# Attention scores with keys on partitions, 512 queries wide, in a one-core decoder layer on Trainium2

## Chip, cores and metric

The kernel runs on 1 core of one Trainium2 chip. The metric is device time in microseconds (us), the median of a kernel's runs. TensorE (PE) multiplies matrices and PEld is its weight load; VectorE (DVE) and ScalarE (ACT) work element by element; GpSimd (POOL) does small work and starts some DMAs; SyncE (SP) starts the others.

## The reference

One decoder layer over 2048 tokens of width 1024, in float32. An input projection feeds two mixers; the change concerns the attention of 8 heads (query and key of 96 numbers, of which 64 are per head and 32 carry the position; value of 64):

```python
h = jnp.einsum('bsd,dn->bsn', x, w_in[l]) + b_in[l]
for start in range(0, seq, Q_BLOCK):
    end = start + Q_BLOCK
    s = jnp.einsum('bqhd,bkhd->bhqk', q[:, start:end], k[:, :end]).astype(jnp.float32) * scale
    causal = jnp.arange(end)[None, :] <= (start + jnp.arange(Q_BLOCK))[:, None]
    p = jax.nn.softmax(jnp.where(causal, s, -jnp.inf), axis=-1)
    outs.append(jnp.einsum('bhqk,bkhd->bqhd', p.astype(v.dtype), v[:, :end]))
```

The attention output is gated by SiLU, the other mixer is a gated spatial unit, both are projected, gated, added, projected again and normalised.

## The kernel before

Every float32 product runs as three passes of the type float32r: `split` (lines 64 to 66) makes a 12-bit head of an operand on ACT (`hi`) and the remainder on DVE (`lo`), and hi·hi, hi·lo and lo·hi add up in one PSUM bank (`mm3`).

Four stages follow each other. Stage 1 makes q, k and v of all tokens and stores their heads and remainders in DRAM; stage 2 makes the mixed v of the spatial unit; stage 3 is attention; stage 4 gates, merges, projects and normalises (lines 774 to 873). The gates' own projections (`gates`, lines 493 to 568, tile `psg`) are cut into steps of three 512-wide products. The first 48 steps run ahead of stage 3, all others between the steps of the attention, as filling work that depends on nothing of it.

Stage 3 (from line 575) goes through 64 blocks of 256 queries of a head (`Block`). A block has three kinds of steps. `score` (line 619) puts 128 queries on the partitions and up to 512 keys in columns of a bank `pss`, three passes each; DVE adds the causal mask and takes each row's maximum (lines 631 to 639); when a row of 128 queries is complete, ACT takes the exponential with the maximum as its bias and adds up the row (line 642). `turn` (line 648) transposes the probabilities on TensorE, two key tiles and 256 queries at a time, into the bank `pt`, and `split` turns them into `ph` and `pl`. `product` (line 670) multiplies these with V, whose 128 columns hold head and remainder, into `po`; lines 684 to 686 add the two halves and send the block to DRAM. The row sums stay in `ls`; after all blocks they are turned, inverted and written to `rd` (lines 756 to 764), and stage 4 loads them back as `r` and multiplies (lines 816 to 818).

The order on TensorE is written by a loop (lines 715 to 754) that models when each step's input should be ready; `FILL` sets how much gates' work stands between. Within stage 3 TensorE keeps that order, and every engine takes its own instructions in the order in which they stand:

```python
            elif turned and turned[0][0] <= now and (blocks[vi].kv > 0 or o_free <= now):
                cost = blocks[vi].product(lo)
            elif ti < si and ti <= vi + 1 and done_s[ti] <= now and t_ready <= now and len(turned) < 2:
                cost = blocks[ti].turn()
            elif si < len(order) and si <= ti + 1 and banks and banks[0] <= now:
                cost, last = blocks[si].score()
            if cost:
                credit += cost * FILL
            else:
                next(fill, None)
```

Loads of Q (lines 603 and 604), K and V (lines 588 to 590) and gates' weights (`fst`, line 498) share SP's queue; POOL starts the stores `gd` and `otd`.

Of the kernel before, what the change touches and what calls it, by code (L numbers as in the profile page):

```python
# [19 lines left out]
ALU = mybir.AluOpType  # L20
# [13 lines left out]
W = 512           # width of each mixer  # L34
C = 512           # tokens of a chunk
# [6 lines left out]
# inv_freq[i] = 10000 ** (-2 i / 32) in float32  # L42
# [10 lines left out]
LAG_S, LAG_E, LAG_H, LAG_T, LAG_O = 1500.0, 700.0, 1500.0, 2100.0, 1500.0  # L53
FILL = 1.19       # time of the gates' products per time of the attention's
# [3 lines left out]
def hybrid_layer_kernel(ctx, tc, xT, x, pos, invf, w_lat, b_lat, w_v, b_v,  # L58
# [41 lines left out]
    rd = dram.tile([H, S], F32, name="rd")  # L100

    # ----------------------------------------------------------- constants
# [7 lines left out]
    # keep where q - k >= 0  # L110
# [7 lines left out]
    # x^T, two chunks of tokens on chip, each as (hi, lo)  # L118
# [22 lines left out]
    # ======================================================= 1: q, k and v  # L141
# [10 lines left out]
    # latent weights, with the first chunk of x  # L152
# [20 lines left out]
    # rope tables: cos, sin of pos * inv_freq for all tokens  # L173
# [24 lines left out]
    # cos(r) = sin(pi/2 - |r|)  # L198
# [6 lines left out]
    # up projections, with the rms gains (and the score scale) folded in  # L205
# [8 lines left out]
    tc.keep_in_program_order(dve.tensor_scalar(gq, gq, SCALE, None, op0=ALU.mult))  # L214
    for t in range(3):
# [11 lines left out]
    def rope(dst, src, t0, n, heads, nm):  # L227
        """dst[P, n*heads, 32] = rope(src); tables of token tiles t0 .. t0+n"""
# [16 lines left out]
    def latent(c, ts):  # L245
        """latents of token tiles ts: bias, rms norm, rope of k"""
# [44 lines left out]
    def up(c, lh, ll):  # L291
        """k, v and q of a chunk, in four parts"""
# [4 lines left out]
        evict(pk, DR, krd[:, :, tok])  # L297
# [11 lines left out]
        for t in range(4):  # L309
            tk = slice(t * P, (t + 1) * P)  # L310
            # q rope
# [8 lines left out]
            # k nope, head pairs  # L320
# [4 lines left out]
            # v  # L325
# [10 lines left out]
            # q nope, head pairs  # L336
# [24 lines left out]
    # ============================== 2: v of the spatial gating unit, mixed  # L361
    with ExitStack() as ph:
# [12 lines left out]
        def gelu_v(c, t):  # L375
            """gelu(v) of a token tile and its mean and variance"""
# [21 lines left out]
        # the first tiles along with the last part of phase 1  # L398
# [27 lines left out]
            # [s, g, t]: keep t >= s  # L426
# [148 lines left out]
    with ExitStack() as ph:  # L575
# [17 lines left out]
        class Block:  # L593
# [4 lines left out]
            def __init__(self, h, qc, hds):  # L598
# [6 lines left out]
                if h not in hds:  # L605
                    hds[h] = head(h)
# [108 lines left out]
        while vi < len(order):  # L715
# [3 lines left out]
            elif turned and turned[0][0] <= now and (blocks[vi].kv > 0 or o_free <= now):  # L719
                lo = len(turned[0]) == 1  # L720
                turned[0].pop(0)
                if lo:
                    turned.pop(0)
# [210 lines left out]
```

## Time and profile before

| | us |
|---|---|
| median of 3 runs | 1771.89 |
| lowest and highest run | 1771.39, 1774.26 |
| span of the profiled execution, first to last instruction | 1775.5 |
| TensorE busy in that span | 1731.4 (98%) |
| VectorE, ScalarE, GpSimd busy | 1094.2 (62%), 754.6 (43%), 134.3 (8%) |

The profiled execution has no time of its own beside its span of 1775.5 us, which is 0.2% above the median of the runs. In the profile, a group of instructions is one line with its engine, operation, tiles (written from left to right as out<-in), shape and count, then busy time, the mean duration of one in ns, and the idle time of its engine just before, with what ended it. Products on TensorE overlap: a 512-wide one lasts some 390 ns, but the next begins sooner, so that their pace is read from the starts in the timeline. The granted clock is a share of 2.4 GHz; 0.5 would be 1.2 GHz throughout.

### The profile page before, as it was taken

How to read it: one execution, taken by the hardware profiler on the slowest of the kernel's cores; microseconds unless marked ns; L12 is line 12 of the kernel's file. 1: busy time of each engine (PE TensorE's matmuls, PEld its weight loads, DVE VectorE, ACT ScalarE, POOL GpSimd, SP SyncE). 2: the span in 40 equal slices, each digit the busy share in tenths (PEclk: the TensorE clock that was granted, in tenths of full speed). 3: DMA queues.
4: the chain of work that ended last, by engine and by line, in shares of the span. 5: the costliest groups of instructions: out<-in, count | busy, mean ns of one | idle time of the engine just before them, and what ended most of it. 6: DMA issues, size and time to landing. Idle time of an engine off the chain costs nothing.

```text
span 1775.5 us, 25048 instructions
## 1 busy us (share of the span) xinstructions
PE 1731.4 (98%) x9249; PEld 1484.1 (84%) x9249; DVE 1094.2 (62%) x2209; ACT 754.6 (43%) x1708; POOL 134.3 (8%) x231
## 2 busy tenths in 40 slices
PE   7999999899999999999999999999999999999998
PEld 7999887788888888888788888888888877888886
DVE  6765686476664555444776666654445478777664
ACT  6533442255544454545655445544544341303020
POOL 0000011100000100000100000100001000000000
PEclk9999999999999999999999999999999999999999
DMA  6564851631321422422713212321123886657341
GB/s 220 194 196 160 276 170 38 181 99 49 101 72 66 140 68 66 119 68 75 215 62 89 76 55 81 122 72 59 60 66 120 283 270 225 215 197 215 120 131 72
DMA packets 111100, 229.06 MB, mean 129 GB/s; under 512 B 13120, under 2 KB 41920, under 8 KB 108608
## 3 DMA queue, kind: packets, MB, share of 16 engines
q1 hardware_dynamic: 99968, 193.88, 34.9%
q0 software_dynamic: 11008, 33.57, 5.4%
q8 instruction: 73, 1.20, 0.3%
q14 instruction: 51, 0.42, 0.1%
HBM read 155.50 MB, written 71.89 MB: 128 GB/s over the span
## 4 chain that ended last, share of the span: by engine, by line
PE 45%; issue 41%; DMA 5%; POOL 4%; DVE 3%; ACT 2%; SPq 0%; POOLq 0%; DVEq 0%; ACTq 0%
PE po L86 11%; PE psg L86 9%; PE psa L86 4%; PE psl L86 4%; PE pb L86 4%; PE pa L86 4%; PE pss L86 3%; PE pt L658 2%; POOL gd L519 2%; DMA wost<-in_w_out_dram 1%; PE psq L86 1%; POOL otd L686 1%; DMA xst<-in_xT_dram 1%; DMA mxd<-mo 1%; PE psr L86 1%
## 5 line engine op out<-in xcount | busy, mean ns | idle before, releaser
L86 PE MATMUL psg<-xh,fwh 128*128 128x512 f32 x896 | 375.3, 419 | 4.9 <-DVE fo L522 4.9
L66 DVE TENSOR_TENSOR pl<-pt,ph 128x512 fp32r<-128x512 f32 (+2 forms) x352 | 199.7, 567 | 287.2 <-ACT ph L65 285.5
L86 PE MATMUL psg<-xl,fwh 128*128 128x512 f32 x896 | 354.5, 396 | 0.0
L86 PE MATMUL psg<-xh,fwl 128*128 128x512 f32 x896 | 354.1, 395 | 0.0
L65 ACT CAST ph<-pt 128x512 fp32r<-128x512 f32 (+2 forms) x352 | 172.0, 489 | 241.4 <-PE pt L658 208.8
L642 ACT ACTIVATE pr<-pss,nm 128x512 f32<-128x512 f32 (+2 forms) x320 | 198.0, 628 | 114.9 <-DVE nm L639 95.9
L86 PE MATMUL pss<-Kh,Q 96*128 96x512 f32 (+3 forms) x640 | 222.5, 377 | 12.9 <-DMA Q<-qrd 7.2
L86 PEld LDWEIGHTS psg<-xh,fwl 128*128 128x128 f32 x896 | 169.6, 189 | 38.4
L636 DVE TENSOR_REDUCE mx<-pss 128x1 f32<-128x384 f32 (+2 forms) x288 | 175.6, 619 | 29.4 <-PE pss L86 26.1
L86 PEld LDWEIGHTS psg<-xh,fwh 128*128 128x128 f32 x896 | 170.6, 190 | 25.6 <-issue 5.3
L86 PEld LDWEIGHTS psg<-xl,fwh 128*128 128x128 f32 x896 | 171.4, 191 | 20.7
L658 PE MATMUL pt<-ident,pr 128*128 128x128 f32 x1088 | 167.2, 274 | 0.0
L86 PEld LDWEIGHTS pss<-Kh,Q 96*128 96x128 f32 x640 | 119.3, 189 | 30.7 <-ACT pr L642 9.7
L658 PEld LDWEIGHTS pt<-ident,pr 128*128 128x128 f32 x1088 | 125.6, 141 | 5.8 <-ACT pr L642 0.4
L86 PEld LDWEIGHTS po<-ph,V 128*128 128x128 f32 x576 | 108.7, 189 | 26.0 <-ACT ph L65 3.2
L86 PE MATMUL pss<-Kl,Q 96*128 96x512 f32 (+2 forms) x320 | 115.9, 362 | 0.0
L86 PE MATMUL po<-pl,V 128*128 128x256 f32 x576 | 113.9, 279 | 0.2
L86 PE MATMUL po<-ph,V 128*128 128x256 f32 x576 | 112.8, 276 | 1.2 <-DVE o L685 0.7
L86 PEld LDWEIGHTS po<-pl,V 128*128 128x128 f32 x576 | 96.5, 190 | 11.3 <-DVE pl L66 1.2
L86 PE MATMUL po<-woh,mh 128*128 128x512 f32 x256 | 100.8, 394 | 1.2 <-ACT mh L65 1.2
L86 PE MATMUL po<-woh,ml 128*128 128x512 f32 x256 | 100.4, 393 | 0.0
L86 PE MATMUL po<-wol,mh 128*128 128x512 f32 x256 | 99.7, 390 | 0.0
(208 smaller groups left out, 2986.3 us busy)
## 6 DMA issues: line engine op xcount, KB each, us to landing
fst<-in_w_feat_dram SPq DMA_DIRECT2D x56, 512.0 KB, 3.7
gd<-fo POOLq DMA_DIRECT2D x96, 256.0 KB, 2.3
wabst<-in_w_ab_dram SPq DMA_DIRECT2D x32, 512.0 KB, 4.2
xst<-in_xT_dram SPq DMA_DIRECT2D x31, 512.0 KB, 4.9
kd<-e SPq DMA_DIRECT2D x16, 512.0 KB, 3.2
vd<-ve SPq DMA_DIRECT2D x16, 512.0 KB, 4.1
qnd<-e SPq DMA_DIRECT2D x16, 512.0 KB, 4.7
Q<-qnd SPq DMA_DIRECT2D x64, 128.0 KB, 2.9
```

What stands on the lines that cost most here:

```text
L65: act.copy(hi, src)
L66: dve.tensor_tensor(lo, src, hi.bitcast(F32), op=ALU.subtract)
L86: inorder(pe.matmul(*args, **kw))
L519: pool.dma_start(gd[c][m], o)
L636: dve.tensor_reduce(self.mx[:, i:i + 1], ps[:, :n], axis=AX.X, op=ALU.max)
L642: act.activation(pr[:, k0:k0 + ne], pe_[:, :ne], AF.Exp, bias=self.nm, accum_out=ls[:, self.h, 2 * self.qc + j, e:e + 1])
L658: inorder(pe.transpose(pt[:, i, j * P:(j + 1) * P], self.pr[j][:, (k + i) * P:(k + i + 1) * P], ident))
L686: pool.dma_start(otd[self.qc // 2][self.h * DV:(self.h + 1) * DV, self.qc % 2 * 256:(self.qc % 2 + 1) * 256], o2)
```

## The change

Stage 3 is rewritten for 32 blocks of 512 queries (8 heads, four chunks c of 512 tokens; the block of chunk c has 4(c+1) key tiles of 128). Each product of the score has 128 keys on the partitions and 512 queries in columns (`score`, bank `pst`), so that the exponential leaves the probabilities as the product with V wants them. The maximum of a query, which lies across partitions there, comes from an earlier product of its own, `top`: heads of q times heads of k, one pass, queries on the partitions, in banks `pss`; DVE masks and reduces it. When all `top` steps of a block are done, DVE spreads the negated maxima on a diagonal (`dg`), `shift` multiplies that with a matrix of ones (bank `pbm`), and ACT writes the result as row 96 of the block's Q; K has a row of ones there (`krd`). The row sums are added on POOL into `acc`, tile by tile; `total` sums them over partitions with another product with ones (bank `pbl`), DVE inverts, scales the block's output and POOL stores it. The path through `rd` and `r` is gone. A block's `top` steps stand between the `score` steps of the block before it.

```diff
-    krd = dram.tile([DR, 2, S], F32, name="krd")
+    krd = dram.tile([DR + 1, 2, S], F32, name="krd")
...
+    one = xs.tile([P, 2, C], F32, tag="st", name="one")
+    dve.memset(one[:1, 0, :], 1.0)
+    dve.memset(one[:1, 1, :], 0.0)
+    for c in range(4):
+        sp.dma_start(krd[DR:, :, c * C:(c + 1) * C], one[:1])
...
+        ps_s = ph.enter_context(tc.tile_pool(name="p3S", bufs=2, space=PSUM))
+        ps_t = ph.enter_context(tc.tile_pool(name="p3T", bufs=2, space=PSUM))
+        ps_b = ph.enter_context(tc.tile_pool(name="p3B", bufs=1, space=PSUM))
...
+            Kt = kp.tile([DH + 1, 2, S], F32R, tag="K", name="K")
...
+            for ks in (slice(0, 512), slice(512, S)):
+                sp.dma_start(Kt[:DN, :, ks].bitcast(F32), kd[h // 2, h % 2 * DN:(h % 2 + 1) * DN, :, ks])
+                sp.dma_start(Kt[DN:, :, ks].bitcast(F32), krd[:, :, ks])
...
+                self.Qt = kp.tile([DH + 1, 2, C], F32R, tag="Q", name="Q")
+                sp.dma_start(self.Qt[:DN].bitcast(F32), qnd[h // 2, h % 2 * DN:(h % 2 + 1) * DN, :, cs])
+                sp.dma_start(self.Qt[DN:DH].bitcast(F32), qrd[h // 4, h % 4 * DR:(h % 4 + 1) * DR, :, cs])
...
+                for j in range(4):
+                    nb = 4 * c + j + 1
+                    ends = [-(-nb * (i + 1) // (c + 1)) * P for i in range(c + 1)]
+                    self.units += [(j, i, k0, k1 - k0, i == c)
+                                   for i, (k0, k1) in enumerate(zip([0] + ends, ends))]
...
+            def top(self):
+                j, i, k0, n, last = self.units.pop(0)
                 ps = ps_s.tile([P, 512], F32, tag="s", name="pss")
...
-                mm(ps[:, :n], Qh, self.Kh[:, ks], start=True, stop=False)
-                mm(ps[:, :n], Qh, self.Kl[:, ks], start=False, stop=False)
-                mm(ps[:, :n], Ql, self.Kh[:, ks], start=False, stop=True)
...
-                        act.activation(pr[:, k0:k0 + ne], pe_[:, :ne], AF.Exp, bias=self.nm,
-                                       accum_out=ls[:, self.h, 2 * self.qc + j, e:e + 1])
...
-                        inorder(pe.transpose(pt[:, i, j * P:(j + 1) * P],
-                                             self.pr[j][:, (k + i) * P:(k + i + 1) * P], ident))
+                mm(ps[:, :n], self.Qt[:DH, 0, j * P:(j + 1) * P], self.Kt[:DH, 0, k0:k0 + n],
+                   start=True, stop=True)
                 with tc.high_priority():
                     if last:
...
+                        dve.tensor_tensor(ps[:, n - P:n], ps[:, n - P:n], mask, op=ALU.add)
+                    dve.tensor_reduce(self.mx[:, j, i:i + 1], ps[:, :n], axis=AX.X, op=ALU.max)
+                    if not self.units:
+                        nm = sm.tile([P, 4, 1], F32, tag="nm", name="nm")
+                        dve.tensor_reduce(nm, self.mx, axis=AX.X, op=ALU.max, negate=True)
+                        self.dg = sm.tile([P, 4, P], F32R, tag="dg", bufs=1, name="dg")
+                        dve.tensor_tensor(self.dg, ident.unsqueeze(1).to_broadcast([P, 4, P]),
+                                          nm.to_broadcast([P, 4, P]), op=ALU.mult)
...
+            def shift(self):
+                pb = ps_b.tile([P, C], F32, tag="b", name="pbm")
+                mm(pb, ones, self.dg.rearrange("p j q -> p (j q)"), start=True, stop=True)
+                with tc.high_priority():
+                    act.copy(self.Qt[DH:, 0, :], pb[DH:DH + 1, :])
...
+            def score(self, k):
+                q0 = max(0, k - 4 * self.c) * P
+                ks = slice(k * P, (k + 1) * P)
+                ps = ps_t.tile([P, C], F32, tag="t", name="pst")
+                mm(ps[:, q0:], self.Kt[:, 0, ks], self.Qt[:, 0, q0:], start=True, stop=False)
+                mm(ps[:, q0:], self.Kt[:DH, 1, ks], self.Qt[:DH, 0, q0:], start=False, stop=False)
+                mm(ps[:, q0:], self.Kt[:DH, 0, ks], self.Qt[:DH, 1, q0:], start=False, stop=True)
+                p = pp.tile([P, C], F32, tag="p", name="p")
+                hi = pp.tile([P, C], F32R, tag="ph", name="ph")
+                lo = pp.tile([P, C], F32R, tag="pl", name="pl")
+                with tc.high_priority():
+                    if k >= 4 * self.c:
+                        dve.tensor_tensor(ps[:, q0:q0 + P], ps[:, q0:q0 + P], maskt, op=ALU.add)
+                    act.activation(p[:, q0:], ps[:, q0:], AF.Exp)
+                    split(p[:, q0:], hi[:, q0:], lo[:, q0:])
+                    if k == 0:
+                        self.acc = sm.tile([P, C], F32, tag="acc", name="acc")
+                        pool.tensor_copy(self.acc, p)
...
+                        pool.tensor_tensor(self.acc[:, q0:], self.acc[:, q0:], p[:, q0:], op=ALU.add)
+                    if k == self.nk - 1:
+                        self.ah = sm.tile([P, C], F32R, tag="ah", bufs=1, name="ah")
+                        self.al = sm.tile([P, C], F32R, tag="al", bufs=1, name="al")
+                        split(self.acc, self.ah, self.al)
...
+            def product(self, k, e):
...
+                mm(self.po[:, q0:], self.Vt[:, k, :], (hi, lo)[e][:, q0:],
+                   start=k == 0 and e == 0, stop=k == self.nk - 1 and e == 1)
+                if k == self.nk - 1 and e == 1:
...
+                        act.copy(o1, self.po[DV:, :])
+                        dve.tensor_tensor(self.o2, self.po[:DV, :], o1, op=ALU.add)
...
+            def total(self):
+                pb = ps_b.tile([P, C], F32, tag="b", name="pbl")
+                mm(pb, ones, self.ah, start=True, stop=False)
+                mm(pb, ones, self.al, start=False, stop=True)
+                r = sm.tile([DV, C], F32, tag="r", bufs=1, name="r")
+                dve.reciprocal(r, pb[:DV, :])
+                dve.scalar_tensor_tensor(self.o2, self.o2, 0.5, r, op0=ALU.mult, op1=ALU.mult)
+                pool.dma_start(otd[self.c][self.h * DV:(self.h + 1) * DV, :], self.o2)
...
-        order = [(h, qc if h % 2 == 0 else 7 - qc) for h in range(H) for qc in range(8)]
...
+        order = [(h, c if h % 2 == 0 else 3 - c) for h in range(H) for c in range(4)]
...
+        def work(cost):
+            credit[0] += cost * rate
+            while credit[0] > 0.5 * STEP_NS:
+                credit[0] -= STEP_NS
+                next(fill, None)
...
+        work(blocks[0].shift())
+        todo, sums = [], []
+        def later():
+            if len(todo) > 2:
+                n, k = todo.pop(0)
+                b = blocks[n]
+                work(b.product(k, 0))
+                work(b.product(k, 1))
+                if k == b.nk - 1:
+                    sums.append(n)
+            elif sums:
+                work(blocks[sums.pop()].total())
...
+        for n in range(len(order)):
+            b, nx = blocks[n], blocks.get(n + 1)
+            for k in range(b.nk):
+                work(b.score(k))
+                todo.append((n, k))
+                if sums:
+                    work(blocks[sums.pop()].total())
+                later()
+                if nx:
+                    want = min(nx.nu, -(-nx.nu * (k + 1) // max(1, b.nk - 1 - b.nk // 5)))
+                    while nx.nu - len(nx.units) < want:
+                        work(nx.top())
+            if nx:
+                work(nx.shift())
+            block(n + 2)
+        while todo:
+            n, k = todo.pop(0)
+            work(blocks[n].product(k, 0))
+            work(blocks[n].product(k, 1))
+        work(blocks[len(order) - 1].total())
...
-                for e in range(2):
-                    sp.dma_start(r[e * DV:(e + 1) * DV, :], rd[2 * f + e, tok].partition_broadcast(DV))
-                dve.tensor_tensor(o, o, r, op=ALU.mult)
```

TensorE in stage 3, before, where probabilities are turned; `psg` is a gates' product, `pt` a transpose of probabilities `pr`, `po` a product with V:

```order
L86 MATMUL po<-ph,V 128x256 x2
L86 MATMUL po<-pl,V 128x256 x2
L658 MATMUL pt<-ident,pr 128x128 x4
L86 MATMUL psg<-xh_2940,fwh 128x512
L86 MATMUL psg<-xl_2941,fwh 128x512
```

Between a gates' step and the products with V stands a turn of four transposes.

TensorE after the change, some steps within a block; `pst` is a score with keys on partitions, `pss` a `top` product of the next block:

```order
L86 MATMUL pst<-Q,K 128x512 x3
L86 MATMUL psg<-xh_2972,fwh 128x512
L86 MATMUL psg<-xl_2973,fwh 128x512
L86 MATMUL psg<-xh_2972,fwl 128x512
...
L86 MATMUL po<-ph,V 128x512
L86 MATMUL po<-pl,V 128x512
...
L86 MATMUL pss<-K,Q 128x512 [waits DVE_49] x2
```

No transpose of probabilities is left on TensorE, and one-pass products `pss` have come in.

TensorE after the change, at the end of a block without a gates' step behind `pbm`:

```order
L86 MATMUL pst<-Q,K 128x128 [waits Activation_49]
L86 MATMUL pst<-Q,K 128x128 x2
L86 MATMUL po<-ph,V 128x384 [waits Activation_49]
L86 MATMUL po<-pl,V 128x384 [waits DVE_49]
L86 MATMUL psg<-xh_2972,fwh 128x512
L86 MATMUL psg<-xl_2973,fwh 128x512
L86 MATMUL psg<-xh_2972,fwl 128x512
L86 MATMUL pbm<-dg,ones 128x512 [waits PE_49]
L86 MATMUL pst<-Q,K 128x512 [waits DVE_49,Activation_49]
```

ACT at the same place:

```order
L668 ACTIVATE p<-pst 128x128 [waits DVE_49,Pool_49]
L65 CAST ph<-p 128x128 [waits PE_49,Activation_49]
L65 CAST ah<-acc 128x512 [waits Pool_49]
L652 CAST Q<-pbm 1x512 [waits DMAHW7_49,DMAHW0_49,PE_49]
L668 ACTIVATE p<-pst 128x512 [waits PE_49]
```

The first score of the next block waits for ACT's write of Q's row 96 (`Q<-pbm`), and ahead of that on ACT stands the head of the finished sums (`ah`), which waits for POOL.

DVE after the change, in a block of chunk 0, from the inverse of the block before to the diagonal of the next:

```order
L702 RECIPROCAL r<-pbl 64x512 [waits PE_49]
L637 TENSOR_TENSOR pss<-pss,mask 128x128 [waits PE_49]
L667 TENSOR_TENSOR pst<-pst,maskt 128x128 [waits PE_49]
L638 TENSOR_REDUCE mx<-pss 128x1 [waits DVE_49]
L703 SCALAR_TENSOR_TENSOR o_6250<-o_6250,r 64x512
L641 TENSOR_REDUCE nm<-mx 128x4 [waits DVE_49]
L66 TENSOR_TENSOR pl<-p,ph 128x128 [waits Activation_49]
L643 TENSOR_TENSOR dg<-ident,nm 128x512 [waits DVE_49]
```

The inverse stands ahead of the last mask of this block and of the diagonal that `shift` needs.

## Rows read from the trace of the kernel before

**Rows 1.** The profile's page: span, and busy time of each engine.

```profile
span 1775.5 us, 25048 instructions
...
PE 1731.4 (98%) x9249; PEld 1484.1 (84%) x9249; DVE 1094.2 (62%) x2209; ACT 754.6 (43%) x1708; POOL 134.3 (8%) x231
```

**Rows 2.** Busy time by stretch: end of attention, all of it; then stage 4.

```profile
core 0: us, PE busy (x) PEld busy (x) DVE busy (x) ACT busy (x) POOL busy (x), PEclk, DMA share, GB/s
...
1366.00:1411.50 45.50, 45.50 (x203) 37.74 (x203) 23.27 (x34) 15.83 (x25) 4.88 (x9) 1.00 0.87 294
353.60:1411.50 1057.90, 1043.53 (x5745) 904.39 (x5744) 612.32 (x1237) 535.62 (x1307) 85.22 (x156) 1.00 0.30 94
...
1500.00:1700.00 200.00, 200.00 (x880) 164.85 (x879) 143.78 (x221) 41.50 (x54) 8.25 (x9) 1.00 0.57 184
```

**Rows 3.** Groups of TensorE's instructions by shape, 353.6 to 1411.5 us.

```profile
L86 PE MATMUL psg<-xh,fwh 128*128 128x512 f32 x848 | 355.1, 419 | 0.0
...
L658 PE MATMUL pt<-ident,pr 128*128 128x128 f32 x1088 | 167.2, 274 | 0.0
```

**Rows 4.** TensorE's timeline: start, length, instruction, count in the row.

```profile
503.24 0.40 PE L86 MATMUL po<-pl,V 128*128 128x256 f32 x2
503.48 0.60 PE L658 MATMUL pt<-ident,pr 128*128 128x128 f32 x4
503.83 0.48 PE L86 MATMUL psg<-xh,fwh 128*128 128x512 f32 x1
504.15 0.40 PE L86 MATMUL psg<-xl,fwh 128*128 128x512 f32 x1
504.38 0.39 PE L86 MATMUL psg<-xh,fwl 128*128 128x512 f32 x1
504.61 0.34 PE L86 MATMUL pss<-Kh,Q 96*128 96x384 f32 x1
504.79 0.33 PE L86 MATMUL pss<-Kl,Q 96*128 96x384 f32 x1
...
515.95 0.49 PE L658 MATMUL pt<-ident,pr 128*128 128x128 f32 x3
516.19 0.48 PE L86 MATMUL pss<-Kh,Q 96*128 96x512 f32 x1
516.50 0.39 PE L86 MATMUL pss<-Kl,Q 96*128 96x512 f32 x1
```

**Rows 5.** Waits of TensorE, 353.6 to 1411.5 us: total, times, longest.

```profile
PE pss L86 <- DMA Q<-qrd: 7.2, 3, 3.1
PE pss L86 <- ACT pr L642: 5.4, 6, 2.2
```

**Rows 6.** Busy time by stretch around TensorE's longest wait of stage 3.

```profile
608.00:612.00 4.00, 0.87 (x8) 0.67 (x7) 1.12 (x3) 1.00 (x3) 0.54 (x1) 1.00 0.91 242
612.00:616.00 4.00, 4.00 (x13) 3.33 (x12) 1.85 (x4) 1.45 (x4) 0.00 (x0) 0.57 0.15 45
616.00:620.00 4.00, 4.00 (x30) 3.84 (x28) 3.19 (x10) 1.36 (x4) 0.53 (x1) 1.00 0.65 218
```

**Rows 7.** Groups of VectorE's instructions by shape, whole span.

```profile
L66 DVE TENSOR_TENSOR pl<-pt,ph 128x512 fp32r<-128x512 f32 x224 | 154.5, 690 | 227.6 <-ACT ph L65 226.5
...
L631 DVE TENSOR_TENSOR pss<-pss,mask 128x128 f32<-128x128 f32 x128 | 36.7, 293 | 16.2 <-PE pss L86 15.0
...
L763 DVE RECIPROCAL r<-pl 128x128 f32<-128x128 f32 x1 | 1.0, 957 | 1.1 <-PE pl L761 1.1
```

**Rows 8.** Groups of ScalarE's instructions by shape, whole span.

```profile
L65 ACT CAST ph<-pt 128x512 fp32r<-128x512 f32 x224 | 131.2, 586 | 165.5 <-PE pt L658 162.2
...
L65 ACT CAST fwh<-fst 128x512 fp32r<-128x512 f32 x112 | 66.7, 622 | 38.0 <-PE psg L86 37.6 <-DMA fst<-in_w_feat_dram 0.4
...
L642 ACT ACTIVATE pr<-pss,nm 128x128 f32<-128x128 f32 x8 | 2.9, 367 | 3.4 <-DVE nm L634 3.4
```

**Rows 9.** Groups of GpSimd's instructions by shape, whole span.

```profile
L427 POOL TENSOR_SCALAR_AFFINE_SELECT wsst<-wsst 128x1024 f32<-128x1024 f32 x1 | 1.1, 1099 | 20.5 <-DMA wsst<-in_wsT_dram 20.5
L106 POOL TENSOR_SCALAR_AFFINE_SELECT ident<-ident 128x128 f32<-128x128 f32 x1 | 0.3, 292 | 0.6 <-DVE ident L105 0.6
```

More of the change, by code (lines that the diff above doesn't have):

```diff
@@ L52 @@
 MT_ORDER = [m for f in range(4) for m in (MT_U + f, MT_ZB + f, MT_ZA + f)] + list(range(MT_GA, MT))
[L53 to L54 removed]
+MM_NS = 0.45
+STEP_NS = 3 * MM_NS * 512
 @with_exitstack
@@ L581, in hybrid_layer_kernel @@
+        ps_b = ph.enter_context(tc.tile_pool(name="p3B", bufs=1, space=PSUM))
         ps_o = ph.enter_context(tc.tile_pool(name="p3O", bufs=1, space=PSUM))
+        maskt = sm.tile([P, P], F32, bufs=1, name="maskt")
+        dve.memset(maskt, 0.0)
+        pool.affine_select(out=maskt, in_=maskt, compare_op=ALU.is_ge, fill=NEG,
+                           base=0, pattern=[[1, P]], channel_multiplier=-1)
+        ones = sm.tile([P, P], F32R, bufs=1, name="ones")
+        dve.tensor_scalar(ones, ident, 0.0, 1.0, op0=ALU.mult, op1=ALU.add)
@@ L590, in head @@
             sp.dma_start(Vt.bitcast(F32), vd[h])
[L591 removed]
+            return Kt, Vt
         class Block:
[L598 to L617 removed]
@@ L690, in hybrid_layer_kernel @@
-        ls = sm.tile([P, H, NT, 4], F32, tag="ls", bufs=1, name="ls")
-        dve.memset(ls, 0.0)
-        keep[0] = True
-        order = [(h, qc if h % 2 == 0 else 7 - qc) for h in range(H) for qc in range(8)]
-        hds = {}
-        blocks = [None] * len(order)
-        done_s = [0.0] * len(order)
-        si = ti = vi = 0
-        now = credit = 0.0
-        banks = [0.0] * 4
-        row, turned = [], []
-        t_ready = o_free = act_free = 0.0
+                        dve.tensor_tensor(ps[:, n - P:n], ps[:, n - P:n], mask, op=ALU.add)
@@ L706, in block @@
+        keep[0] = True
+        order = [(h, c if h % 2 == 0 else 3 - c) for h in range(H) for c in range(4)]
+        hds = {0: head(0)}
+        blocks = {}
         def block(n):
-            if n < len(order) and blocks[n] is None:
-                h, qc = order[n]
-                if n % 8 == 1 and h + 1 < H:
+            if n < len(order):
+                h, c = order[n]
+                blocks[n] = Block(h, c, hds)
+                if n % 4 == 1 and h + 1 < H:
                     hds[h + 1] = head(h + 1)
-                blocks[n] = Block(h, qc, hds)
@@ L713, in hybrid_layer_kernel @@
-        block(0)
-        block(1)
-        while vi < len(order):
-            cost = 0.0
-            if credit > 0.0:
-                pass
[L719 to L723, printed above, removed]
-                cost = blocks[vi].product(lo)
-                if blocks[vi].kv == blocks[vi].nk:
-                    vi += 1
-                    o_free = now + cost + LAG_O
-            elif ti < si and ti <= vi + 1 and done_s[ti] <= now and t_ready <= now and len(turned) < 2:
-                cost = blocks[ti].turn()
-                t_ready = now + cost + LAG_T
-                turned.append([now + cost + LAG_H, t_ready])
-                if blocks[ti].kt == blocks[ti].nk:
-                    ti += 1
-            elif si < len(order) and si <= ti + 1 and banks and banks[0] <= now:
-                cost, last = blocks[si].score()
-                banks.pop(0)
-                row.append(now + cost)
-                if last:
-                    act_free = max(now + cost + LAG_S, act_free)
-                    for _ in row:
-                        act_free += LAG_E
-                        banks.append(act_free)
-                    done_s[si] = act_free + 200.0
-                    row = []
-                if not blocks[si].todo:
-                    si += 1
-                    block(si + 1)
-            if cost:
-                credit += cost * FILL
-            else:
-                cost = 648.0
-                credit -= cost
-                next(fill, None)
-            now += cost
@@ L757, in hybrid_layer_kernel @@
-        l1 = sm.tile([P, H * NT], F32, tag="l1", bufs=1, name="l1")
-        dve.tensor_reduce(l1, ls.rearrange("p h b i -> p (h b) i"), axis=AX.X, op=ALU.add)
-        dve.tensor_scalar(l1, l1, 2.0, None, op0=ALU.mult)
-        pl1 = ps_t.tile([P, P], F32, tag="t", name="pl1")
-        pe.transpose(pl1, l1, ident)
-        r1 = sm.tile([P, P], F32, tag="r1", bufs=1, name="r1")
-        dve.reciprocal(r1, pl1)
-        sp.dma_start(rd.rearrange("h (b q) -> (h b) q", q=P), r1)
+        cols = sum((4 * c + 2.5) * 4 * P + 3 * C + 5 * (4 * c * C + 1280) for h, c in order)
@@ new lines, in hybrid_layer_kernel @@
+        rate = (len(MT_ORDER) * 4 * 8 - 48 - 24) * STEP_NS / (cols * MM_NS)
+        credit = [0.0]
+        def work(cost):
[3 more added lines that the diff above has]
+                next(fill, None)
+        block(0)
+        while blocks[0].units:
+            work(blocks[0].top())
+            work(300.0)
+        for _ in range(6):
+            next(fill, None)
+        work(blocks[0].shift())
+        todo, sums = [], []
```

109 lines of the change are left out of this document (23 added, 86 removed).

## The prediction

> **What bounds the kernel now.** The page first: TensorE is busy 1731.4 of 1775.5 us and no other engine above 62% [rows 1]. Busy time hides pace, so the stretches come next: attention takes 1057.9 us at a granted clock of 1.00, with VectorE at 612.3 (58%), ScalarE at 535.6 and GpSimd at 85.2 [rows 2]. Its last 45.5 us hold nothing but gates' products. In stage 4 there are 880 products in 200 us, 0.227 each. The timeline gives the paces inside attention from start to start [rows 4]: 0.23 us for 512 columns, 0.17 for 384, 0.12 for 256, and by proportion 0.06 for 128. A turn of four transposes costs 0.67 to the second start behind it, less the 0.23 of the product between: 0.44; one of three costs 0.55 less 0.23, 0.32.
>
> With these, stage 3 adds up so: 3 x 848 gates' products [rows 3] are 585.1 us, the scores (three passes over 139,264 columns) 188.5, the products with V 128.5, the turns (1088 transposes [rows 3], 224 fours and 64 threes) 119.0. That is 1021.1, so 36.8 of the 1057.9 is idle or slow. The list of waits names some of it: 7.2 for Q's loads and 5.4 for the exponential [rows 5]. The longest gap shows the rest: after some 3 us with 8 products the clock of the next 4 us is 0.57, and 13 products run where the following 4 us hold 30 [rows 6]. So a wait of 3 us costs about 2 us more afterwards.
>
> **Columns on TensorE, removed and added.** The transposes go: -119.0. The scores keep their columns (672 products of 512, 96 each of 384, 256 and 128: 188.4) and the V products are 448 of 512 and 64 of each narrower width, 125.6: together -3. New are 320 `top` products in one pass (139,264 columns, 62.9), 32 `shift` (7.4) and 64 `total` (14.7): +85. Net **-37**.
>
> **The old stalls.** They hang on turns and on short blocks. Half as many blocks, each with its Q loaded two blocks ahead, and scores that wait for nothing but two banks should keep about 11 of the 36.8 (late loads, where SP's queue is shared as before). **-26.**
>
> **The added wait at each block's end.** This is the price I trust least, and it decides. The first score of the next block needs row 96 of Q. Ahead of that write ScalarE has the cast `ah`, which needs GpSimd's last add, which needs the last exponential. From the start of the last score, with durations of the nearest rows: 0.35 for its passes to end, mask 0.29 [rows 7], exponential 0.37 [rows 8], GpSimd's add of 128 columns about 0.35 (from 0.29 [rows 9]), cast 0.6, and the write of Q taken like the 0.59 of a PSUM cast [rows 8], with 0.25 for five hand-overs: **2.8 us**. Meanwhile TensorE has the narrow score (0.19), two V products (0.35), three gates' products (0.69) and `pbm` (0.23), 1.46 us; in about half of these 24 boundaries three more gates' products, 2.14. The waits are 1.35 and 0.66: 12 x 1.35 + 12 x 0.66 = **+24**. Bounds: 14, if the Q write of one partition is short, to 48, if the chain takes 3.8.
>
> **Blocks of chunk 0.** They have four key tiles, so between `total` of the block before and their own last `top` lies little. On VectorE the inverse stands ahead of the last mask and of `dg`. An inverse over 128 x 128 took 0.957 us [rows 7]; 0.15 of that taken as fixed, 512 columns take 0.15 + 4 x 0.80 = 3.4. Bounds 1.36 (if half of the partitions counted) to 3.83 (four times). From `total` to `shift` TensorE has 3.7 us of work by the paces; VectorE needs 0.7 for what is before it, 3.4 and 2.6 for masks, reduction, scale, `pl` and `dg`: 6.7. So `shift` waits 2.9 and the score behind it another 0.6: 3.5 for each of seven, **+24.5** (10 to 35), and since gaps this long are followed by half clock [rows 6], **+6**.
>
> **Smaller waits.** Where chunk 1 follows chunk 0 (4 times), `top` steps stand three in a row on two banks, and the third waits for a mask and a reduction, about 1.5: **+6**. The inverse in the other 24 blocks holds reductions that free `pss`: 7 in all (0 to 30). Q's loads still come just in time once or twice: 4, against 7.2 before [rows 5]. Stage 4 loses cover: where 45.5 us of gates' work lay ahead of it [rows 2], only 48 products, 11 us, do now: 4 (0 to 10). Together **+21**.
>
> **Hidden work.** VectorE gets 128 masks more (37 by 0.293), 32 `dg` and 32 scalings like `pl` (22 each by 0.690 [rows 7]), 5 for `nm` and 109 for the inverses: +195, so some 807 us of about 1070, 75%. ScalarE has one exponential and one head for a tile where it had the same, with 32 `ah` and 32 Q writes (38) on top: near 55%. GpSimd gets 320 adds and copies; the nearest rows are selects, 1.099 for 1024 columns and 0.292 for 128 [rows 9]. An add of 512 columns lies between 0.64 (interpolated) and 1.1 (it reads 1024): at most 350 us on an engine that was busy 85. All three stay below TensorE, so nothing for their sums; if VectorE's cover goes, it is case C. The path through `rd` (32 loads, 16 multiplications) goes from stage 4, where nothing waited for it that I count: 0.
>
> The Trainium skill ("GPSIMD Engine Reference", section "Performance versus the Vector engine") gives 2.6 cycles an element at 1.2 GHz for such an add; my estimate from that page is 1.1 us for 512 columns, the upper of my two ends, and no row here shows it. By it the sum would not move, as GpSimd would be at a third.
>
> **Sum.** -37 - 26 + 24 + 24.5 + 6 + 6 + 7 + 4 + 4 = **+12.5**. The sum is made on the span of 1775.5, which is 0.2% above the median of the runs; put on the median of 1771.9 it gives **1784 us**.
>
> **Rivals.** *B: faster, the new waits are covered.* For it: TensorE's columns fall for certain, and of the hand-over's terms only mask and cast are measured on tiles like these. If the chain takes 2.1 us or less, boundaries with six gates' products no longer wait, and the others wait 0.66; if the inverse costs 1.4, chunk 0 waits little. Taking 0.66 at all 24 is 16, with 10 for chunk 0 and 4 for stage 4: 30. -63 + 30 = -33, **1739**. It decides below a chain of 2.1 us and an inverse of 1.5. Against it: five hand-overs over four engines in a row, and 0.957 for a quarter of the columns.
>
> *C: slower, VectorE falls behind for GpSimd.* `pl` had one input in PSUM (`pt`) and one in SBUF; now both, `p` and `ph`, are in SBUF, while GpSimd adds the same `p`. If the two engines can't read at once, a `pl` that becomes ready 0.6 us into an add of 1.1 waits 0.5: 320 x 0.5 = 160 us on VectorE, 967 of 1070 (90%). A key tile has 3.3 us of TensorE work and VectorE would then have 0.3 us free in it; reductions free `pss` late, and the chains at block ends grow by 0.5 to 1 us: 32 x 0.8 = 26, with 14 for `top` steps: **1824**. It decides when the wait per tile exceeds VectorE's free 0.8 us. For it: nothing in the trace of before puts these two side by side. Against: GpSimd would hold the port a third of the time only.
> The Trainium skill ("SBUF — State Buffer", section "Who interferes with whom") states that a VectorE instruction with two SBUF inputs and a GpSimd instruction that reads SBUF lock each other out, the second waiting until the first is done; it is the mechanism of C and speaks against this change. No run here shows it yet; the profile after would, by `pl` instructions longer than 0.69.
>
> *That the transposes stay in some form* is excluded by the order of TensorE after the change.
>
> **Chances and range.** The forecast (A, 1765 to 1805 as its own range): 0.42; B 0.30; C 0.28. The measurement tells some 3.5 us (0.2%) from no change. Of A 0.05 lies below 1768.4, 0.09 within 3.5 of the median, 0.28 above; B is all faster, C all slower: faster 0.35, same 0.09, slower 0.56. For 8 in 10 the range must take in the upper part of B and most of C; with the inverse at 1.36 and the boundary waits at 14 A's sum falls by 25 or more, with 48 and 35 it rises by 35: 1736 to 1832.
>
> **What would show it.** Right: TensorE's waits for ScalarE's Q write and for `dg` sum to 40 to 60 us and lead its list; the inverse lasts 3 us or more; stage 3 is 1060 to 1080 us; the clock dips at the chunk-0 blocks alone. For B: stage 3 under 1035, inverse under 1.5, chain under 2.1. For C: `pl` above 0.9 on average, VectorE above 88%, and waits of TensorE for `mx` spread over the blocks. Wrong altogether: waits on loads or at stage 4 that outweigh these, or paces of `top` products other than 0.23.

## The result, and the profile after

| | before | after |
|---|---|---|
| median of the runs, us | 1772.7 (1771.39 to 1774.26) | 1885.49 (1879.17 to 1894.78) |
| span of the profiled execution, us | 1775.5 | 1877.5 |

The changed kernel is slower: ratio 1.063, 95% interval 1.060 to 1.067. The sign was forecast; the size was not: 12.5 us stood in the sum, 113 were measured, and 1885 lies above the range. The profiled execution is the fastest of the changed kernel's four, so that what follows accounts for 102 of the 113.

The page's first lines answer to [rows 1]: TensorE is busy 93% of the span where it was 98%, VectorE 74% where it was 62%.

```profile
span 1877.5 us, 22826 instructions
...
PE 1742.6 (93%) x8064; PEld 1434.4 (76%) x8064; DVE 1383.8 (74%) x2321; ACT 764.9 (41%) x1388; POOL 486.1 (26%) x520
```

Busy time by stretch (columns as in [rows 2]), cut at the last gates' product as there: attention, then stage 4.

```profile
353.60:1501.00 1147.40, 1045.65 (x4534) 850.18 (x4533) 889.70 (x1327) 539.22 (x977) 435.76 (x443) 0.96 0.25 79
1501.00:1877.50 376.50, 357.56 (x1537) 289.55 (x1535) 256.23 (x388) 79.48 (x102) 15.39 (x17) 0.98 0.57 185
```

Attention is 89.5 us longer (1057.9 before [rows 2]), stage 4 12.5 (364.0 before). The 89.5 can be put together from three things. TensorE stands idle 101.8 us (1147.4 less 1045.7) where it was 14.4: +87. Its granted clock is 0.96 where it was 1.00: attention lost 44 us to half clock, in 20 stretches, where it had lost 5 in three: about +40. And the products that the change saves are the -37 of the forecast. 87 + 40 - 37 = 90. This is rougher than it looks: some 4 us of half clock lie in time that is also counted as idle, the changed attention begins at 345.7 us, so that some 6 us of its products lie ahead of the cut, and about 10 us of busy time stay unexplained.

The waits of TensorE, 353.6 to 1490 us, name the idle time (total, times, longest):

```profile
PE pst L86 <- ACT Q L652: 61.2, 27, 4.0
PE pbm L86 <- DVE dg L643: 20.5, 8, 4.2
PE pss L86 <- DVE mx L638: 11.1, 12, 1.9
PE pbm L86 <- DVE r L702: 6.4, 1, 6.4
PE po L86 <- DVE pl L66: 2.0, 5, 0.9
```

88 of the 101 are the hand-over between blocks (Q's row 96, `dg`, and once the single bank that `pbm` and `pbl` share, which the inverse still read): 86 at the 31 block ends, 2 at the first block's start. Groups by shape, VectorE first, then ScalarE and GpSimd:

```profile
L66 DVE TENSOR_TENSOR pl<-p,ph 128x512 fp32r<-128x512 f32 x224 | 228.6, 1023 | 146.1 <-ACT ph L65 145.0
L66 DVE TENSOR_TENSOR fwl<-fst,fwh 128x512 fp32r<-128x512 f32 x112 | 100.5, 907 | 10.4 <-ACT fwh L65 10.3
L702 DVE RECIPROCAL r<-pbl 64x512 f32<-64x512 f32 x32 | 106.9, 3341 | 1.7 <-PE pbl L86 1.7
L66 DVE TENSOR_TENSOR al<-acc,ah 128x512 fp32r<-128x512 f32 x32 | 22.1, 692 | 11.7 <-ACT ah L65 11.7
...
L652 ACT CAST Q<-pbm 1x512 fp32r<-1x512 f32 x32 | 18.5, 578 | 11.3 <-PE pbm L86 10.7
...
L674 POOL TENSOR_TENSOR acc<-acc,p 128x512 f32<-128x512 f32 x192 | 267.5, 1393 | 320.7 <-ACT p L668 319.6
L674 POOL TENSOR_TENSOR acc<-acc,p 128x128 f32<-128x128 f32 x32 | 18.6, 581 | 48.8 <-ACT p L668 48.5
```

The inverse took 3.34 us (3.4 forecast) and the Q write 0.58 (0.59 forecast, and one partition made it no shorter). But `pl` of 512 columns took 1.02 us where it took 0.69 [rows 7], with the same count; `al`, of the same form, took 0.69; none of its 32 ran beside an add of GpSimd. And GpSimd's add took 1.39 us, above my upper bound of 1.1.

One block end shows the hand-over. TensorE's timeline (start, length):

```profile
439.93 0.45 PE L86 MATMUL pst<-Q,K 97*128 97x128 f32 x3
...
441.78 0.40 PE L86 MATMUL pbm<-dg,ones 128*128 128x512 f32 x1
445.69 0.80 PE L86 MATMUL pst<-Q,K 97*128 97x512 f32 x1 [3.51 <-ACT Q L652]
```

VectorE and then ScalarE in the same time:

```profile
441.90 0.70 DVE L66 TENSOR_TENSOR pl<-p,ph 128x256 fp32r<-128x256 f32 x1 [0.30 <-ACT ph L65]
442.52 0.68 DVE L549 SCALAR_TENSOR_TENSOR fo<-ft,fo 128x512 f32<-128x512 f32 x1
443.12 0.29 DVE L667 TENSOR_TENSOR pst<-pst,maskt 128x128 f32<-128x128 f32 x1
...
443.50 0.28 ACT L668 ACTIVATE p<-pst 128x128 f32<-128x128 f32 x1 [1.10 <-DVE pst L667]
443.81 0.30 ACT L65 CAST ph<-p 128x128 fp32r<-128x128 f32 x1
444.41 0.62 ACT L65 CAST ah<-acc 128x512 fp32r<-128x512 f32 x1 [0.30 <-POOL acc L674]
445.06 0.58 ACT L652 CAST Q<-pbm 1x512 fp32r<-1x512 f32 x1
```

The last score is done at 440.4, but its mask starts at 443.12: on VectorE the `pl` of the tile before and a gates' step stand ahead, and that `pl` itself waited for the tile before it, whose mask was late as well. From the mask on, the chain takes what was forecast, 2.5 us to the end of the Q write. Over the 24 ends of chunks 1 to 3 the mask starts 0.5 to 3.1 us after the score is done, 1.7 in the mean, and the next block's score 4.3.

A few instructions earlier in the same queue, `gu` (of the gates) and `dg` took 1.59 and 1.47 us. Both have two inputs in SBUF, and both began while GpSimd was adding (GpSimd's timeline, then VectorE's):

```profile
434.76 2.45 POOL L674 TENSOR_TENSOR acc<-acc,p 128x512 f32<-128x512 f32 x1 [3.56 <-ACT p L668]
438.70 1.02 POOL L674 TENSOR_TENSOR acc<-acc,p 128x384 f32<-128x384 f32 x1 [1.49 <-ACT p L668]
...
436.18 1.59 DVE L543 SCALAR_TENSOR_TENSOR gu<-ft,fo 128x512 f32<-128x512 f32 x1
438.81 1.47 DVE L643 TENSOR_TENSOR dg<-ident,nm 128x512 fp32r<-128x512 f32 x1
```

Each ends some 0.55 us after the add does. So do 115 of the 124 `pl` of 512 columns that begin inside an add; these 124 take 1.28 us in the mean, while the 86 that meet no add or copy of GpSimd take 0.68.

What TensorE's wait at this end leaves behind stands in the stretches of 4 us around it (clock: third value from the right):

```profile
436.00:440.00 4.00, 4.00 (x22) 3.29 (x20) 3.93 (x7) 1.12 (x3) 2.24 (x2) 1.00 0.37 121
...
444.00:448.00 4.00, 2.31 (x6) 1.85 (x7) 1.07 (x2) 1.90 (x4) 0.94 (x2) 0.71 0.17 66
448.00:452.00 4.00, 4.00 (x18) 3.37 (x17) 1.94 (x3) 0.97 (x2) 0.60 (x1) 0.86 0.01 4
```

Also VectorE was busy 3.93 of the 4 us before that end: its share of 78% over the stage is no measure of a block's last tiles, where masks, `dg` and `pl` meet. The clock was half after 13 of the 24 ends of chunks 1 to 3 and after six of the seven of chunk 0. The length of the wait alone did not decide it: an end with a wait of 1.7 us was followed by half clock, one with a wait of 2.8 us was not.

### The profile page after: what moved, and what is told of

Same layout as the page of the kernel before. It is cut to its first block, busy times and chain, and to the rows that moved or that the text cites. A ratio compares the mean times of both kernels' runs of the same rounds, so it can differ in the third digit from the quotient of the medians.

```text
span 1877.5 us, 22826 instructions
## 1 busy us (share of the span) xinstructions
PE 1742.6 (93%) x8064; PEld 1434.4 (76%) x8064; DVE 1383.8 (74%) x2321; ACT 764.9 (41%) x1388; POOL 486.1 (26%) x520
## 4 chain that ended last, share of the span: by engine, by line
PE 63%; DVE 20%; ACT 6%; issue 5%; DMA 4%; POOL 1%; SPq 0%; ACTq 0%; DVEq 0%; POOLq 0%
PE psg L86 19%; PE po L86 13%; PE pst L86 8%; DVE pl L66 5%; PE psl L86 5%; PE pa L86 4%; PE pb L86 4%; PE psa L86 4%; DVE mx L638 3%; DVE r L702 3%; PE pss L86 2%; ACT p L668 2%; ACT ph L65 2%; DMA gd<-fo 2%; DVE fwl L66 2%
## 5 line engine op out<-in xcount | busy, mean ns | idle before, releaser
L674 POOL TENSOR_TENSOR acc<-acc,p 128x512 f32<-128x512 f32 (+3 forms) x288 | 347.7, 1207 | 470.9 <-ACT p L668 469.2
L66 DVE TENSOR_TENSOR pl<-p,ph 128x512 fp32r<-128x512 f32 (+1 forms) x320 | 292.4, 916 | 184.0 <-ACT ph L65 182.5
L668 ACT ACTIVATE p<-pst 128x512 f32<-128x512 f32 (+1 forms) x320 | 170.7, 533 | 475.7 <-PE pst L86 232.5
L86 PE MATMUL pst<-Q,K 97*128 97x512 f32 (+3 forms) x960 | 261.3, 382 | 61.2 <-ACT Q L652 61.2
L86 PEld LDWEIGHTS pst<-Q,K 96*128 96x128 f32 (+1 forms) x960 | 180.6, 198 | 105.0 <-ACT Q L652 73.7
L638 DVE TENSOR_REDUCE mx<-pss 128x1 f32<-128x512 f32 (+2 forms) x320 | 186.8, 597 | 15.2 <-PE pss L86 13.0
L65 ACT CAST ph<-p 128x512 fp32r<-128x512 f32 (+1 forms) x320 | 178.1, 556 | 9.0
L86 PE MATMUL pss<-K,Q 96*128 96x512 f32 (+2 forms) x320 | 114.0, 379 | 13.8 <-DVE mx L638 11.1
L86 PE MATMUL po<-pl,V 128*128 128x512 f32 (+1 forms) x320 | 119.1, 372 | 2.1 <-DVE pl L66 2.0
L86 PE MATMUL po<-ph,V 128*128 128x512 f32 (+1 forms) x320 | 117.6, 367 | 0.3
```

The source lines that it names most:

```text
L65: act.copy(hi, src)
L66: dve.tensor_tensor(lo, src, hi.bitcast(F32), op=ALU.subtract)
L86: inorder(pe.matmul(*args, **kw))
L638: dve.tensor_reduce(self.mx[:, j, i:i + 1], ps[:, :n], axis=AX.X, op=ALU.max)
L668: act.activation(p[:, q0:], ps[:, q0:], AF.Exp)
L674: pool.tensor_tensor(self.acc[:, q0:], self.acc[:, q0:], p[:, q0:], op=ALU.add)
```

## Experiments

All times are medians, and a gain is the difference from the changed kernel's 1885.5. Its four executions spread over 16 us, and the kernel before measured 1772.7 to 1776.2 beside these runs, so a gain is good to some 5 us. Ratios are to the kernel before on the same chip. The theories: H, the hand-over at block ends with the clock behind it; L or port, `pl` and GpSimd's adds hold each other up; V, VectorE's queue.

**e1: shift earlier.**

```diff
+                    if b.c and k == b.nk - 2:
+                        work(nx.shift())
-            if nx:
+            if nx and not b.c:
                 work(nx.shift())
```

> Edit: in blocks of chunk 1 to 3 the product `pbm` and ScalarE's write of Q's row 96 stand one key tile earlier, ahead of the block's last score; chunk 0 is as before. Theory H (hand-over: at a block's end the last mask is late on VectorE, so the chain mask, exponential, GpSimd's add, `ah`, Q takes some 4.4 us where 2.8 were forecast, and half clock follows each wait): TensorE's waits for Q fall from 61 us to under 15, the granted clock of stage 3 rises from 0.96 to 0.98 or more, the time falls by 60 to 90 us, to 1795 to 1825. Theory L (VectorE is too slow throughout, because `pl` and GpSimd's adds hold each other up): the waits for Q fall but come back as waits for `mx` and `pl`; the time falls by less than 25, to above 1860.

1848.2 us, a gain of 37, between the two. Waits of TensorE in attention:

```profile
PE pbm L86 <- DVE dg L643: 28.2, 14, 4.2
PE pss L86 <- DMA Q<-qrd: 21.5, 14, 5.3
PE pss L86 <- DVE mx L638: 15.0, 13, 2.6
PE pst L86 <- ACT Q L652: 12.2, 13, 4.4
PE pss L86 <- DMA Q<-qnd: 3.1, 2, 2.5
```

The wait for the Q write went as H said (61 to 12; the one for `dg` and the inverse stayed, 27 to 28), but 25 us of waits for Q's loads came up behind it: with two Q tiles, a block's load is only asked for when the block two before it has ended, and its first `top` comes a tile later.

**e5: the same with three tiles for Q**, each loaded a block earlier (`bufs=3`, `block(n + 3)`).

> Edit: e1_shift_early with three buffers for Q, and each Q loaded one block earlier. In e1 the time fell by 37 us where 60 to 90 were expected, and waits of `top` for Q's loads appeared (24.6 us where none led the list). Theory Q (the loads of Q, asked for only when the block before the last has ended, took over a part of the wait): these waits fall under 5 us, time 1815 to 1832. Theory V (VectorE's backlog sets the pace, and the loads only stand where it would wait anyway): waits for `mx` and `dg` grow by what the loads give, time 1840 to 1855.

1814.6 us. The loads left the list and 34 us came back: Q, not V. Order and loads together are worth 71 us.

**e2: gates' work at the block ends.**

```diff
             if nx:
+                for _ in range(5 if b.c == 0 else 0):
+                    next(fill, None)
                 work(nx.shift())
+                for _ in range(3 if b.c == 0 else 6):
+                    next(fill, None)
```

> Edit: six gates' steps (18 products, 4.1 us) are held back for each boundary and put behind `pbm`, at chunk 0 five ahead of it and three behind; the rest of the gates' work is spread thinner (638 steps where 824 were). Theory H: what is missing is cover of about 4 us at each boundary; the waits for Q and `dg` fall from 88 us to under 25, the clock rises, time 1795 to 1825. Theory L: VectorE's backlog is unchanged and TensorE has less filling work within the blocks, so waits for `mx` and `pl` grow by what the ends gain; time 1860 to 1900.

1807.5 us: H, the best gain of a single edit, 78 us. Waits of TensorE, and the stretch of attention:

```profile
PE pss L86 <- DVE mx L638: 17.4, 16, 2.0
PE pbm L86 <- DVE dg L643: 10.5, 8, 2.3
PE po L86 <- DVE o L693: 9.1, 15, 2.0
...
PE pst L86 <- ACT Q L652: 1.6, 2, 1.3
...
353.60:1432.70 1079.10, 1025.35 (x4535) 829.20 (x4534) 878.95 (x1327) 538.80 (x977) 433.02 (x443) 0.99 0.27 85
```

The waits at block ends fell from 86 to 11 us and the clock of attention rose to 0.99, though the last masks came no earlier (1.9 us after the score is done): the wait was covered, not removed. What L had said happened on a small scale: waits for `mx` rose from 11 to 17 us, and some 19 us of waits for `o`, `pl` and a gates' weight were new.

**e3: mask by a product.**

```diff
...
+                if k >= 4 * self.c:
+                    mm(ps[:, q0:q0 + P], identr, maskr, start=False, stop=False)
...
-                    if k >= 4 * self.c:
-                        dve.tensor_tensor(ps[:, q0:q0 + P], ps[:, q0:q0 + P], maskt, op=ALU.add)
```

> Edit: the causal mask of the scores is added by a 128-column product with the identity in the same bank (128 products, 8 us) and VectorE's 128 masks are gone. Theory H: the exponential of the last tile no longer waits in VectorE's queue; it starts some 0.5 us after its score where it was 2.3 on average, so each of 24 boundaries gains 1.2 to 1.8 us: waits for Q 61 to under 30, with a part of the half clock, less 8 of new products: 1830 to 1860. Theory L: VectorE loses 37 of 882 us of work, which is little: time falls by less than 15, to above 1870.

1842.6 us, 43 gained: H. Waits for Q fell from 61 to 28 with nothing changed behind the mask. At the 24 ends the last exponential starts 0.4 us after its score is done, where it was 2.1; the mask itself is 0.3 of that. So it is VectorE's queue ahead of the mask that had stretched the chain.

**e4: adds left out.** The branch of `pool.tensor_tensor(self.acc...)` runs only for `k == self.nk - 1`.

> Edit: GpSimd's adds of probabilities are left out but for the last key tile of each block, and the first is a memset to one (the row sums are left out of the computation, the chain at the block's end is kept). Theory L: `pl` falls from 1.02 us to 0.69 for 512 columns, VectorE is busy some 90 us less in stage 3, and the time falls by 60 or more, to below 1825. Theory H: `pl` falls likewise, but only what stands ahead of the last mask counts, some 0.3 to 1 us at each boundary: time falls by 10 to 35, to 1850 to 1875, and the waits for Q stay above 40 us.

1818.4 us, 67 gained, which is L's size. `pl` fell to 0.69 and `fwl`, the remainder of a gates' weight, from 0.91 to 0.69:

```profile
L66 DVE TENSOR_TENSOR pl<-p,ph 128x512 fp32r<-128x512 f32 x224 | 153.6, 687 | 178.3 <-ACT ph L65 177.2
L66 DVE TENSOR_TENSOR fwl<-fst,fwh 128x512 fp32r<-128x512 f32 x112 | 75.7, 685 | 12.8 <-ACT fwh L65 12.5
```

The waits for Q fell from 61 to 28, not staying above 40 as H had said. At the 24 ends the mask starts 0.2 us after the score is done, where it was 1.7. So the adds and the late masks are no rivals: the adds are nearly all of what makes the masks late.

**e7: the exponential twice**, so that `pl` reads the bank.

```diff
                     act.activation(p[:, q0:], ps[:, q0:], AF.Exp)
-                    split(p[:, q0:], hi[:, q0:], lo[:, q0:])
+                    act.activation(ps[:, q0:], ps[:, q0:], AF.Exp)
+                    split(ps[:, q0:], hi[:, q0:], lo[:, q0:])
```

> Edit: ScalarE takes each exponential twice, once to SBUF for GpSimd's adds and once in place in the bank; head and remainder are made from the bank, so VectorE's `pl` has one input in SBUF as in the kernel before, and GpSimd's adds are all there. Theory port (`pl` was slow because both its inputs lie in SBUF while GpSimd reads SBUF): `pl` of 512 columns falls from 1.02 to 0.67 to 0.75 us, GpSimd's add from 1.39 towards 1.2; time falls by 20 to 45 us, to 1840 to 1865, though ScalarE has 170 us more and the chain at block ends one exponential more. Theory traffic (GpSimd's work slows VectorE whatever its operands): `pl` stays near 1.0, time 1885 to 1910.

1830.8 us, 55 gained, more than either theory gave. Groups of VectorE and GpSimd:

```profile
L66 DVE TENSOR_TENSOR pl<-pst,ph 128x512 fp32r<-128x512 f32 x224 | 153.1, 684 | 164.8 <-ACT ph L65 160.4 <-PE pss L86 3.9
L66 DVE TENSOR_TENSOR fwl<-fst,fwh 128x512 fp32r<-128x512 f32 x112 | 91.8, 837 | 10.7 <-ACT fwh L65 10.6
...
L675 POOL TENSOR_TENSOR acc<-acc,p 128x512 f32<-128x512 f32 x192 | 266.6, 1389 | 331.1 <-ACT p L668 330.6
```

With all adds in place `pl` is as fast as without them, once one of its inputs lies in PSUM; `fwl`, whose two inputs still lie in SBUF, stays slow (0.84). So it is the second SBUF input, not GpSimd's work as such: of the 113 `pl` that still begin inside an add none ends 0.55 us behind it, and they take 0.69 in the mean. The masks of the 24 ends came 0.4 us after the score instead of 1.7. That the add stayed at 1.39 was a miss of the port theory: `pl` was not what made it slow.

**e8: a quarter of the inverses.**

```diff
-                dve.reciprocal(r, pb[:DV, :])
-                dve.scalar_tensor_tensor(self.o2, self.o2, 0.5, r, op0=ALU.mult, op1=ALU.mult)
+                dve.reciprocal(r[:, :P], pb[:DV, :P])
+                for j in range(0, C, P):
+                    dve.scalar_tensor_tensor(self.o2[:, j:j + P], self.o2[:, j:j + P], 0.5, r[:, :P], op0=ALU.mult, op1=ALU.mult)
```

> Edit: VectorE inverts 128 of a block's 512 row sums and scales all four quarters with them (three quarters of the inverses are left out). Theory V: 107 us of inverses become some 30, the waits for `dg` at chunk 0 (27 us with the one on the inverse) fall under 10, and masks elsewhere come earlier: 1835 to 1860. Theory hidden (outside chunk 0 the inverse lies beside other work): only the waits at chunk 0 go, 1860 to 1875.

1860.7 us, 25 gained, at the edge of both. The inverse fell to 0.94 us and the waits at `pbm` from 27 to 14.5, but those for Q stayed (61, then 65), and the masks at the other 24 ends came no earlier (1.9 us). So outside chunk 0 the inverse is hidden from the hand-over; at chunk 0 it was priced about right. Between the two profiled executions the gain is 16 us, and TensorE's idle time falls by 14 of them.

**e6: e2 and e3 together.**

> Edit: e2_gates_at_ends and e3_mask_on_tensore together. Theory V (what is left in e2, waits for `mx`, `dg`, `o` and `pl`, is VectorE's queue): 37 us less work on VectorE lets these 43 us fall by half or more, time 1775 to 1792. Theory cover (e2 and e3 gain the same waits at the ends of blocks, so they don't add up): 1800 to 1815, the 8 us of new products included.

1794.1 us, between the two: 13 below e2, while e3 alone gave 43. They gain mostly the same waits.

**e9 and e10: all mends, then 48 gates' steps left for stage 4.** e9 has e5, e7, e3, and e2's steps at chunk 0 alone.

> Edit: e5 (shift early, three Q), e7 (exponential twice, `pl` from the bank), e3 (mask on TensorE), and at chunk 0 alone five gates' steps ahead of `pbm` and three behind. Theory sum (hand-over waits, the port and the queue ahead of the mask are separate losses, with the half clock behind them): stage 3 has under 35 us of waits, clock 0.99, time 1740 to 1768, below the kernel before. Theory overlap (all of these edits gain the same waits at block ends, which e6 had down to 7 us already): 1775 to 1800.

> Edit: e9 with 48 more gates' steps (33 us) left for the time between the last V product and stage 4, as the kernel before had it. Theory cover (the start of stage 4 waits for loads and casts that 11 us of gates' work doesn't cover): from the last gates' product to the end 375 us become 362 to 366, time 8 to 12 us below e9, if the thinner filling in stage 3 costs nothing. Theory loss inside (the filling is needed between the steps of attention): 0 to 10 us above e9.

e9: 1768.9 us, ratio to the kernel before 0.997 (0.996 to 0.998), just beyond the upper end of what was expected. e10: **1761.9 us**, 0.993 (0.992 to 0.994), faster than both kernels (0.7% below the kernel before). Its stretches, cut at the last gates' product:

```profile
353.60:1396.00 1042.40, 1020.29 (x4666) 840.52 (x4665) 779.13 (x1214) 664.38 (x1305) 423.36 (x443) 1.00 0.31 93
1396.00:1759.80 363.80, 351.89 (x1535) 287.01 (x1533) 245.37 (x372) 73.90 (x95) 15.37 (x17) 1.00 0.53 174
```

Attention has 22 us idle and full clock, and stage 4 is as long as before the change, where e9 still had 376 us: its 12.5 us had been cover, since 33 us more of gates' work ahead of it took them away.

**e11 and e12: one mend taken back from e10.** e11 has the masks on VectorE again, e12 the single exponential.

> Edit: e10 with the masks of the scores back on VectorE (128 products of 128 columns less on TensorE). Theory V (the order ahead of the last mask still matters): the hand-overs are off the path since `shift` stands early, so what counts is VectorE's 37 us more: waits for `mx` and `dg` grow by 5 to 12 us against 8 us of products less, time 1758 to 1768. Theory done (nothing waits for the mask any more): 8 us below e10, 1752 to 1756.

> Edit: e10 without the second exponential, so `pl` has both inputs in SBUF again; every other mend stays. Theory chain (the port cost time only through late masks and hand-overs at block ends, which e10 covers): within 8 us of e10, 1758 to 1770. Theory pace (VectorE with slow `pl` is late within the blocks too): 20 to 40 us above e10, 1782 to 1802, with waits for `mx` and `pl` of over 30 us.

e11: 1773.6 us, 12 above e10 and outside both expectations, although TensorE has 8 us less to do. Its list has 12.0 us of `pst` waiting for `pl` (1.2 in e10), which reads the bank since e7 and so sets when the next score can have it, and one wait of 9.6 for a gates' weight cast; attention's clock fell to 0.99. Whether the single wait belongs to the edit was not tried. e12: 1775.0 us, 13 above e10, between chain and pace; `pl` is back at 1.00 us. So with the ends covered, the port still costs 13 us where e7 had gained 55; by difference, the rest had gone through the ends of blocks.

## Why the prediction was wrong

- **Products, -37:** right as far as the traces tell. The counts are those of the forecast, and a 512-wide `top` took 0.23 us from start to start, as priced; the pieces of the +89.5 close with it to some 10 us.
- **Old stalls, -26:** half right. The waits named there left the list, but all idle time of before was 14.4 us; the other 12 were to come from slow running, and that grew (see the half clock). The loads of Q also stand twice in the sum, in the 11 kept and in a 4 of their own.
- **The added wait at block ends, +24:** this is the step that failed. Its chain was made of durations, and from the mask on their sum held (2.5 us; the add took 0.58 for 0.35, the exponential 0.28 for 0.37). It took the mask as starting when the score is done, "0.35 for its passes to end, mask 0.29": what stands ahead of the mask on VectorE was put at nothing. I had quoted VectorE's order for a block of chunk 0 alone and priced the inverse there, and not asked what stands ahead at the other ends. There the mask waited 1.7 us in that queue, and the 24 waits summed to 59 us. It is outside the bounds of 14 to 48, because I bounded the chain by durations and not by the queue.
- **Half clock, +6:** it was priced at chunk 0 alone. The longer waits made it follow 19 of the 31 block ends; 40 us, as large a miss as that of the waits. With the ends covered (e2) the clock was 0.99 and in e10 1.00: it was a consequence, not a cause of its own.
- **Chunk 0, +24.5:** about right in size: seven waits, 26.5 us, and an inverse of 3.34.
- **GpSimd at no cost, with C as a rival:** C's mechanism was there, e7 shows it: `pl` 1.02 against 0.68 us. Its place was wrong. I priced it as a backlog over the whole stage (VectorE 90%), and VectorE came to 78% (889.7 of 1147.4). What it did was to push masks back at the ends of blocks, where A's waits were: without the adds (e4) or without the second SBUF input (e7) the masks came 0.2 and 0.4 us after the score instead of 1.7. I had set A and C against each other with a chance for each, but the one lengthens the other. That is why the range, whose upper end took them one at a time, missed.
- **The add of 0.64 to 1.1:** it took 1.39 us, in e7 as well, where `pl` no longer conflicts; here too the bound was too low. GpSimd stayed below 40% of attention; what the longer add cost by itself was not tried.
- **Smaller waits:** `top` waiting for `mx` was 11 us for 6 + 7 forecast. Q's loads did not show, until e1 took away what hid them. Stage 4 was 12.5 for 4, above its bound of 10, and e10 shows that the reason, lost cover, was right.
- **B** would have needed a short chain. e10, where most waits are covered, comes nearest to it: 12 us faster, less than B's 33, with 8 us of mask products and 22 us of idle time left.

The Trainium skill ("SBUF — State Buffer", section "Who interferes with whom") states the rule that e7 tested, and the traces agree: two SBUF inputs beside GpSimd's reads cost `pl` 0.34 us in the mean, one SBUF input nothing, and a `pl` with two that began inside an add ended 0.55 us behind it. The estimate of 1.1 us from "GPSIMD Engine Reference" of the Trainium skill (section "Performance versus the Vector engine") is below the 1.39 measured here; the measurement decides.

## What to carry to other kernels

A chain over engines is not the sum of its durations: ahead of each link write down what stands before it in that engine's own order, and how busy the engine is in just that stretch, not over the stage. Where a hand-over can't be shortened, hold independent work back for it (78 us here), or start it one step earlier and then look at what it had hidden (here loads, 34 us). And two mechanisms that both delay one engine are not alternatives: price them together, here the adds on GpSimd that hold up VectorE and the hand-over that waits for VectorE.

## What the runs showed of the hardware

- A VectorE subtraction of 128x512 with both inputs in SBUF took 1.02 us beside GpSimd's adds, 0.69 without them (e4), and 0.68 beside them with one input in PSUM (e7). Of 124 that began inside an add, 115 ended 0.53 to 0.57 us after it.
- GpSimd's add of 128x512 took 1.39 us, of 128x128 0.58; a copy of 128x512 took 0.63.
- A ScalarE write of one partition by 512 columns took 0.58 us, as much as 128 partitions from PSUM [rows 8].
- A VectorE reciprocal took 0.94 us for 64x128 (e8), 0.96 for 128x128 [rows 7] and 3.34 for 64x512: it goes by columns.
